# Attention scores of two query tiles at a time, in plain float32 on the two row halves of the array

## The chip, the cores and the metric

The kernel runs on one core of a Trainium2 chip. The metric is the device time of one execution in microseconds (us); less is better. Engines are named as in the profile: PE (matrix engine), PEld (its weight loads), DVE (vector), ACT (scalar), POOL (GpSimd), SP (the queue that issues nearly all DMAs).

## What is computed

One layer of a hybrid decoder in float32, for a prompt of 2048 positions and a small sample group. The change is in the prompt's attention: 8 heads of 64 channels; each position looks at keys at distances 0, d, 2d, ... in three branches, each with a softmax of its own, and the branches are merged by their denominators.

```python
BRANCHES = ((128, 1), (512, 4), (2048, 16))      # (window, dilation)
...
s = jnp.einsum('bnqrhc,bnkrhc->bnrhqk', qb, kc).astype(jnp.float32)
s = s * (HEAD_DIM ** -0.5) + bias[None, None, None]
s = jnp.where(valid[None, :, None, None], s, NEG_INF)
lse = jax.nn.logsumexp(s, axis=-1)
p = jnp.exp(s - lse[..., None])
o = jnp.einsum('bnrhqk,bnkrhc->bnqrhc', p.astype(vc.dtype), vc)
...
w = jax.nn.softmax(jnp.stack(lses, axis=0), axis=0)
return jnp.sum(w[..., None] * jnp.stack(outs, axis=0).astype(jnp.float32), axis=0)
```

Before it stands one projection to q, k, v, u, g; behind it the output projection, a gated feed-forward block and norms.

## The kernel before

The program is written out in the order of a plan: `at(step, phase, fn)` registers a call, and calls run by step, then by phase (early, exp, low, scores, turn, mid, values, out, misc, store). Each engine works in the order in which the calls issue its instructions. The projection (steps 0 to 240) stores q and k transposed, as channels by positions, to `qk_d`; each of them is split into a high part, which is rounded for the fast matmul format, and a low rest (L360 on ACT, L361 on DVE), and both parts are stored (L366). Positions of q stand by residue: within a block of 128, those that agree modulo 4 are neighbours. Positions of k stand in their natural order.

The attention follows as a list of items, one per step, from step `B0` = 240 on: for each head 16 band items (a tile of 128 queries against the branches of dilation 1 and 4) and 4 strided items (four residues modulo 16 at once, dilation 16). The orders FIRST, OTHER and LAST say how they are mixed.

- `load_head` (L855) brings three tiles of 128 rows by 2048 per head (L862): `qh` (the high part of q twice), `k` (high part over low part), `ql` (the low part of q twice). `join_q` (L891) adds qh and ql into `qx`, in float32.
- A band item (`band_scores`, L901): near scores, 256 keys, by two matmuls of 128 rows in the fast format, qh and ql against k (L909); far scores, up to 96 keys at distance 4 for each of the four query residues, by four float32 matmuls on 32 columns of the array each (L911). Then the bias and the row's minimum on DVE (L918), the exponential on ACT (L923), three transposes on PE (L934), a copy out (L938 on ACT, L942 on DVE); per four tiles the products with the values (L958 near, L970 far), whose two column halves of the array serve two tiles each.
- A strided item: POOL gathers k and q into `sq` (L985, L986), four float32 matmuls (L994), bias and minimum on DVE (L999, L1001), subtraction on POOL (L1006), exponential on ACT (L1009), four transposes (L1018), values (L1030).
- When a head is done, `Stats` works out the weights of the merge (L1062 is its matmul), stores them (L1090), `merge_load` reads them back spread out over rows (L1104), and POOL merges the outputs in three steps (L1113, L1115, L1117). All this runs beside the items of the next head.

The bias table `b_d` is spread out in DRAM during the projection (`table_spread`, L502). Scores go to one of two buffers `ps_s` of two banks each, of which an item uses the first bank.

Of the kernel before, what the change touches and what calls it, by code (L numbers as in the profile page):

```python
# [13 lines left out]
OP = mybir.AluOpType  # L14
# [53 lines left out]
def hymba_step(ctx: ExitStack, tc: tile.TileContext, A: dict, O: dict):  # L68
# [43 lines left out]
    qk_d = dram.tile([2, 2, DA, T], F32, name="qk_d")  # L112
# [240 lines left out]
    def transposed_split(which, t):  # L353
        pt = zn[which, t]
        thl = zn[which, t] = pair_tile()
        h_, l_ = thl[:, 0], thl[:, 1]
        if which == 0:
            pt = pt.rearrange("p (a i r) -> p a r i", a=4, r=4)
            h_, l_ = (x.rearrange("p (a r i) -> p a r i", a=4, r=4) for x in (h_, l_))
        act.activation(h_, pt, AF.Copy)  # L360
        dve.tensor_sub(l_, pt, h_.bitcast(F32))  # L361
# [129 lines left out]
    def table(c0, n, dst):  # L491
# [3 lines left out]
        act.activation(l_, pt[0:H, 0:n], AF.Copy, scale=-1.0)  # L495
        sync.dma_start(dst, l_)
        if c0 == 0:
            f_ = zn_tile()[0:H, 0:P]
            act.activation(f_, pt[0:H, 3:n:4], AF.Copy, scale=-1.0)
            sync.dma_start(lf_d, f_)  # L500

    def table_spread():  # L502
        for r in range(4):
            rows = slice(r * 32, r * 32 + 32)
            sync.dma_start(b_d[:, rows, 0:FAR], dap(lf_d, 31, [[P, H], [-1, 32], [1, FAR]]))
            sync.dma_start(b_d[:, rows, FAR:BAND], dap(l12_d, 511 - r, [[768, H], [-4, 32], [1, 2 * P]]))
        sync.dma_start(b_d[:, :, BAND:BW], dap(l3_d, 127, [[256, H], [-1, P], [1, P]]))
# [198 lines left out]
    at(70, "turn", table, 0, 512, l12_d[:, 0:512])  # L706
    at(71, "turn", table, 512, 256, l12_d[:, 512:768])
# [139 lines left out]
    def load_values(n, pair, by_residue, n0=0, n1=NT):  # L847

        if by_residue:
            src = dap(v_d, pair * 2 * C, [[NT * DA, P], [DA, NT], [1, 2 * C]])  # L850
        else:
            src = dap(v_d, pair * 2 * C + n0 * P * DA, [[DA, P], [P * DA, n1 - n0], [1, 2 * C]])
        sync.dma_start(n[:, n0:n1].rearrange("p n z c -> p n (z c)"), src)

    def load_head(h):  # L855
# [3 lines left out]
        for nm, w_, parts in (("qh", 0, (0, 0)), ("k", 1, (0, 1)), ("ql", 0, (1, 1))):  # L859
            t_ = d[nm] = qk.tile([P, T], F32R, name=nm, tag="qk", bufs=4)  # L860

            sync.dma_start(t_.bitcast(F32), dap(qk_d, ((w_ * 2 + parts[0]) * DA + h * C) * T,  # L862
                                                [[T, C], [(parts[1] - parts[0]) * DA * T, 2], [1, T]]))
            yield
        d["qx"] = qk.tile([P, T], F32, name="qx", tag="qk", bufs=4)
# [25 lines left out]
    def join_q(h, x, eng):  # L891
        qh, ql, q = (heads[h][nm][:, x * 512:(x + 1) * 512] for nm in ("qh", "ql", "qx"))
        eng.tensor_add(q, qh.bitcast(F32), ql.bitcast(F32))

# [6 lines left out]
    def band_scores(it):  # L901
        d, n = it["d"], it["n"]
        m = min(3, max(0, n - 1))
        near = P if n == 0 else 2 * P
        s = ps_s()[:, 0, :]
        c0 = FAR - 32 * m if n else FAR + P
        k0, f0 = (n + 1) * P - near, (n - 1 - m) * P
        for z, q in ((0, "qh"), (1, "ql")):
            pe.matmul(s[:, BAND - near:BAND], d[q][:, n * P:(n + 1) * P], d["k"][:, k0:k0 + near], start=(z == 0), stop=(z == 1))  # L909
        for r in range(4 if m else 0):  # L910
            pe.matmul(s[r * 32:r * 32 + 32, c0:FAR], d["qx"][:, n * P + r * 32:n * P + r * 32 + 32],  # L911
                      d["k"].bitcast(F32)[:, f0 + r:f0 + r + (32 * m - 1) * 4 + 1:4], start=True, stop=True)
# [68 lines left out]
    def strided_order(h, r4):  # L981

        d = heads[h]
        d["sq", r4] = t_ = ap_.tile([P, 2, 4, P], F32, name="sq", tag="sq", bufs=2)
        pool.tensor_copy(t_[:, 0], d["k"].bitcast(F32).rearrange("p (i r) -> p r i", r=NT)[:, r4 * 4:r4 * 4 + 4])  # L985
        pool.tensor_copy(t_[:, 1].rearrange("p b (n i) -> p b n i", i=8),  # L986
                         d["qx"].rearrange("p (n b i a) -> p b n i a", b=4, i=8, a=4)[:, :, :, :, r4])
# [1559 lines left out]
```

## Time and profile before

| | |
|---|---|
| median of 3 runs | 2467.68 us (2467.61 to 2467.91) |
| the profiled execution, its time | 2464.45 us |
| its span | 2462.6 us |
| mean granted clock of PE in the span | 0.986 |
| HBM read, written | 421.49 MB, 177.38 MB |
| projection | to about 567 us |
| attention of the 8 heads | about 567 to 869 us |
| the rest | about 869 us to the end |

The profile shows one execution. An engine's busy time is the union of its instructions; PE's is near the whole span, so the reader has to look at single items and at what ended the idle time of PE. "Idle before" in a group names who released the engine. The matmul rows hold modelled ends: what one costs is read from start to start. SPq rows are the issues of DMAs, not their transfers.

### The profile page before, as it was taken

Reading aid. Unit: us, or ns where it says so; the run is one execution under the profiler, and the core shown is the slowest. Engines: PE = TensorE matmul, PEld = TensorE weight load, DVE = VectorE, ACT = ScalarE, POOL = GpSimd, SP = SyncE. Lnnn points to the kernel's source line nnn. Section 1 sums busy time; section 2 is a strip of 40 time slices with the busy share of each in tenths; the row PEclk is TensorE's granted clock in tenths of the full one; section 3 lists DMA queues with packets and bytes.
Section 4 is the critical chain, followed back from the end, with each engine's and each line's share of the span. In section 5 each row is a group of like instructions: output and inputs, shape, how many; then the busy total and the mean of one; then the engine's idle time right before and its main releaser. Section 6 shows DMA issues by size and latency. Waiting matters only on the chain. (4 is left out here: it accounts for less than half of the span.)

```text
span 2462.6 us, 42576 instructions
## 1 busy us (share of the span) xinstructions
PE 2385.6 (97%) x14844; PEld 2053.9 (83%) x14844; DVE 1535.3 (62%) x2995; ACT 1204.5 (49%) x2766; POOL 1488.1 (60%) x1196
## 2 busy tenths in 40 slices
PE   8999999999999899999999999999999998999998
PEld 6877786667777678999999988999999977999997
DVE  3468673215666534767777676566666666677676
ACT  6424333224555546666655546444434446555555
POOL 2116553112766737888788764766566663888885
PEclk9999999999999998999999999999999999999999
DMA  9874757887888464787877654767666644877552
GB/s 289 272 230 147 233 158 225 249 285 211 230 219 238 113 199 136 248 267 223 264 248 225 216 160 144 266 201 223 203 212 211 206 136 154 279 246 249 173 169 88
DMA packets 355938, 519.84 MB, mean 211 GB/s; under 512 B 35783, under 2 KB 198784, under 8 KB 350476
## 3 DMA queue, kind: packets, MB, share of 16 engines
q1 hardware_dynamic: 348876, 505.07, 65.5%
q10 hardware_dynamic: 6848, 12.06, 1.7%
q8 instruction: 117, 1.92, 0.3%
q14 instruction: 97, 0.79, 0.1%
HBM read 421.49 MB, written 177.38 MB: 243 GB/s over the span
## 5 line engine op out<-in xcount | busy, mean ns | idle before, releaser
L1664 POOL TENSOR_TENSOR op<-fr,op 128x512 fp32r<-128x512 f32 x392 | 522.4, 1343 | 348.8 <-ACT op L1660 257.5
L1901 PE MATMUL ps_m<-xh,op 128*128 128x384 f32 (+3 forms) x1344 | 429.0, 319 | 4.9 <-DVE raw L1912 3.6
L1902 PE MATMUL ps_m<-xl,op 128*128 128x384 f32 (+3 forms) x1344 | 427.4, 318 | 2.5 <-POOL xl L145 2.5
L1903 PE MATMUL ps_m<-xh,op 128*128 128x384 f32 (+3 forms) x1344 | 427.9, 318 | 0.0
L1754 DVE TENSOR_TENSOR acc<-acc,ps_o 128x512 f32<-128x512 f32 x448 | 300.0, 683 | 72.5 <-PE ps_o L1752 65.2
L1752 PE MATMUL ps_o<-hop 128*128 128x512 f32 x1142 | 322.6, 394 | 1.7 <-DVE hop L1733 1.0
L1901 PEld LDWEIGHTS ps_m<-xh,op 128*128 128x128 f32 x1344 | 255.6, 190 | 14.2 <-DVE raw L1912 6.8
L1902 PEld LDWEIGHTS ps_m<-xl,op 128*128 128x128 f32 x1344 | 255.5, 190 | 8.0 <-POOL xl L145 2.8
L1903 PEld LDWEIGHTS ps_m<-xh,op 128*128 128x128 f32 x1344 | 255.2, 190 | 0.0
L1752 PEld LDWEIGHTS ps_o<-hop 128*128 128x128 f32 x1142 | 209.4, 188 | 37.7 <-DVE hop L1733 2.8
L1660 ACT ACTIVATE op<-fr 128x512 fp32r<-128x512 f32 x396 | 239.5, 621 | 0.0
L325 PE MATMUL ps_s<-wh,xh 128*128 128x512 f32 x480 | 198.0, 413 | 6.4 <-ACT xh L142 6.0
L326 PE MATMUL ps_s<-wl,xh 128*128 128x512 f32 x480 | 191.0, 398 | 0.7 <-DVE wl L233 0.7
L327 PE MATMUL ps_s<-wh,xl 128*128 128x512 f32 x480 | 190.9, 398 | 0.0
L1901 PE MATMUL ps_t<-xh,op 128*128 128x384 f32 (+2 forms) x560 | 180.4, 322 | 6.1 <-ACT xh L1550 3.2
L1902 PE MATMUL ps_t<-xl,op 128*128 128x384 f32 (+2 forms) x560 | 179.5, 321 | 0.7 <-DVE xl L1572 0.7
L1903 PE MATMUL ps_t<-xh,op 128*128 128x384 f32 (+2 forms) x560 | 179.8, 321 | 0.0
L553 POOL TENSOR_TENSOR pr<-kv,qb 96x512 f32<-96x512 f32 x32 | 48.0, 1501 | 169.3 <-DMA kv<-in_cache_k_dram 67.7
L1733 POOL TENSOR_TENSOR hop<-hop 128x512 fp32r<-128x512 f32 x96 | 131.0, 1365 | 11.5 <-ACT hop L1729 6.5
L325 PEld LDWEIGHTS ps_s<-wh,xh 128*128 128x128 f32 x480 | 91.8, 191 | 43.0 <-issue 18.0
L1752 PE MATMUL ps_m<-hop 128*128 128x512 f32 x384 | 119.4, 392 | 0.0
L1901 PEld LDWEIGHTS ps_t<-xh,op 128*128 128x128 f32 x560 | 106.6, 190 | 10.8 <-ACT xh L1550 3.8
(573 smaller groups left out, 5557.6 us busy)
## 6 DMA issues: line engine op xcount, KB each, us to landing
fr<-ab_d SPq DMA_DIRECT2D x308, 256.0 KB
hop<-dd_d SPq DMA_DIRECT2D x143, 256.0 KB
out_ks_dram<-in_cache_k_dram SPq DMA_DIRECT2D x56, 512.0 KB
out_vs_dram<-in_cache_v_dram SPq DMA_DIRECT2D x56, 512.0 KB
ab_d<-fr SPq DMA_DIRECT2D x88, 256.0 KB
dwx<-dd_d SPq DMA_DIRECT2D x71, 256.0 KB
qk_d<-pair SPq DMA_DIRECT2D x64, 256.0 KB
ab_d<-pair SPq DMA_DIRECT2D x63, 256.0 KB
```

Of the source, the lines that this page charges most:

```text
L325: pe.matmul(o[j], xh[:, k, :], wh, start=(k == 0), stop=False)
L326: pe.matmul(o[j], xh[:, k, :], wl, start=False, stop=False)
L327: pe.matmul(o[j], xl[:, k, :], wh, start=False, stop=(k == KD - 1))
L553: eng.tensor_mul(pr[0:n], x[0:n], q[0:n])
L1660: act.activation(ops[f, j][0], ab[f][j], AF.Copy)
L1664: (pool if f > 1 or j in POOL_LOW[f] or B.b0 else dve).tensor_sub(lo_, ab[f][j], hi.bitcast(F32))
L1733: (pool if B.b0 or k >= 7 * (NF // 2 - 1) else dve).tensor_sub(lo_, lo_.bitcast(F32), hi.bitcast(F32))
L1752: pe.matmul(ps, l_, r_, start=(new and y == 0), stop=(y == 2), skip_group_check=True)
L1754: dve.tensor_add(x[:, cs], x[:, cs], ps)
L1901: pe.matmul(out, wh[:, ks], xh[:, :, k], start=(k == 0 and q not in (2, 4, 6)), stop=False, skip_group_check=True)
L1902: pe.matmul(out, wh[:, ks], xl[:, :, k], start=False, stop=False, skip_group_check=True)
L1903: pe.matmul(out, wl[:, ks], xh[:, :, k], start=False, stop=(k == 3), skip_group_check=True)
```

## The change

Exact q and k of 64 channels are stored once (`qk_d` is half as large; L360 stays as a copy, L361 goes), both by residue. A head loads two tiles, q and k, each with its 64 channels twice, on rows 0 to 63 and 64 to 127. `pair_scores` issues the scores of two neighbouring tiles: the even tile on the rows 0 to 63 of the array and into the first bank of `ps_s`, the odd one on the rows 64 to 127 and into the second bank. The near scores are one float32 matmul per tile (256 keys), the far scores four. A strided item puts its four matmuls on the two halves in turn, with two banks; its bias takes two DVE instructions. `join_q` goes. As k now stands by residue, the columns of the bias table and the rows of the near values do too: the table is spread by 36 smaller transfers, one per step, and a natural-order value load takes four DMAs instead of one. The bias of an even tile comes right before that of the odd one, the transposes of both come one step later than before, and the groups' value products two steps later; the tile `e` gets 6 buffers instead of 3.

```diff
-        thl = zn[which, t] = pair_tile()
-        h_, l_ = thl[:, 0], thl[:, 1]
...
-        act.activation(h_, pt, AF.Copy)
-        dve.tensor_sub(l_, pt, h_.bitcast(F32))
+        zn[which, t] = x = pair_tile(F32)[:, 0]
+        act.activation(x.rearrange("p (a r i) -> p a r i", a=4, r=4), pt.rearrange("p (a i r) -> p a r i", a=4, r=4), AF.Copy)
...
-    at(75, "misc", table_spread)
+    for j in range(36):
+        at(84 + j, "misc", table_spread, j // 9, j % 9 - 1)
...
-            src = dap(v_d, pair * 2 * C + n0 * P * DA, [[DA, P], [P * DA, n1 - n0], [1, 2 * C]])
...
+        for r in range(4):
+            src = dap(v_d, (n0 * P + r) * DA + pair * 2 * C, [[4 * DA, 32], [P * DA, n1 - n0], [1, 2 * C]])
+            sync.dma_start(n[r * 32:r * 32 + 32, n0:n1], src)
...
-        for nm, w_, parts in (("qh", 0, (0, 0)), ("k", 1, (0, 1)), ("ql", 0, (1, 1))):
-            t_ = d[nm] = qk.tile([P, T], F32R, name=nm, tag="qk", bufs=4)
...
+        for w_, nm in enumerate("qk"):
+            t_ = d[nm] = qk.tile([P, T], F32, name=nm, tag="qk", bufs=2)
+            sync.dma_start(t_, dap(qk_d, (w_ * DA + h * C) * T, [[0, 2], [T, C], [1, T]]))
             yield
-        d["qx"] = qk.tile([P, T], F32, name="qx", tag="qk", bufs=4)
...
-        for z, q in ((0, "qh"), (1, "ql")):
-            pe.matmul(s[:, BAND - near:BAND], d[q][:, n * P:(n + 1) * P], d["k"][:, k0:k0 + near], start=(z == 0), stop=(z == 1))
-        for r in range(4 if m else 0):
-            pe.matmul(s[r * 32:r * 32 + 32, c0:FAR], d["qx"][:, n * P + r * 32:n * P + r * 32 + 32],
-                      d["k"].bitcast(F32)[:, f0 + r:f0 + r + (32 * m - 1) * 4 + 1:4], start=True, stop=True)
...
+    def pair_scores(*its):
+
+        d, s = its[0]["d"], ps_s()
+        for z, it in enumerate(its):
+            n = it["n"]
+            m = min(3, max(0, n - 1))
+            near = P if n == 0 else 2 * P
+            it.update(s=s[:, z, :], c0=FAR - 32 * m if n else FAR + P, m=m)
+            half = slice(z * C, z * C + C)
+            k0 = (n + 1) * P - near
+            pe.matmul(it["s"][:, BAND - near:BAND], d["q"][half, n * P:(n + 1) * P], d["k"][half, k0:k0 + near], start=True, stop=True)
+        for r in range(4):
+            for z, it in enumerate(its):
+                n, m, half = it["n"], it["m"], slice(z * C, z * C + C)
+                if m:
+                    k = d["k"][half].rearrange("p (n r i) -> p n r i", r=4, i=32)[:, n - 1 - m:n - 1, r, :]
+                    c = n * P + r * 32
+                    pe.matmul(it["s"][r * 32:r * 32 + 32, it["c0"]:FAR].rearrange("p (n i) -> p n i", i=32),
+                              d["q"][half, c:c + 32], k, start=True, stop=True)
...
+            half = slice(a % 2 * C, a % 2 * C + C)
+            pe.matmul(s[:, a % 2, a // 2 * P:(a // 2 + 1) * P], t_[half, 1, a], t_[half, 0, a], start=True, stop=True)
...
-        dve.tensor_tensor(e, s.rearrange("p (a b) -> p a b", a=4), d["b3"].unsqueeze(1).broadcast_to([P, 4, P]), op=OP.add)
+        for y in range(2):
+            dve.tensor_tensor(e[:, 2 * y:2 * y + 2], s[:, y], d["b3"].unsqueeze(1).broadcast_to([P, 2, P]), op=OP.add)
...
-    LAST = [0, "s", 1, "s", 2, "s", 3, "s", 4, 5, 6, 7] + list(range(8, NT))
+    LAST = ["s", 0, 1, "s", 2, 3, "s", 4, 5, "s", 6, 7] + list(range(8, NT))
...
-                grp["y"] = (4, 5, 6) if h in (0, H - 1) else (4, 6, 7)
+                grp["y"] = (4, 5, 6) if h == H - 1 and n == NT - 1 else (6, 7, 8)
...
-        at(x + 1, "scores", bias, it)
+        if it["kind"] == "s" or n % 2:
+            at(x + 1, "scores", bias, it)
+        else:
+            x += 1 if items[i + 1]["kind"] == "b" else 2
+            at(x + 1, "low", bias, it)
```

How the order moves on PE, in the middle of a head (`e` holds probabilities, `ps_t` and `ps_o` are banks for transposes, `sq` is the strided copy). Before:

```order
L909 MATMUL ps_s<-k,qh 128x256
L909 MATMUL ps_s<-k,ql 128x256
L911 MATMUL ps_s<-k,qx 32x96 x4
L1018 MATMUL ps_t_5680<-ident,e_5583 128x128 x4
L934 MATMUL ps_t_5687<-ident,e 128x128 x3
L994 MATMUL ps_s<-sq 128x128 x4
L934 MATMUL ps_o_5705<-ident,e 128x128 x3
L909 MATMUL ps_s<-k,qh 128x256
L909 MATMUL ps_s<-k,ql 128x256
L911 MATMUL ps_s<-k,qx 32x96 x4
L934 MATMUL ps_t_5722<-ident,e 128x128 x3
```

The same place on PE in the changed kernel (L899 near, L906 far, L1015 and L928 transposes, L964 far values, L989 strided scores):

```order
L899 MATMUL ps_s<-k,q 128x256 x2
L906 MATMUL ps_s<-k,q 32x96 x8
L1015 MATMUL ps_o_5702<-ident,e_5625 128x128 x4
L964 MATMUL ps_o_5672<-pt,vf 64x32 x8
L989 MATMUL ps_s<-sq 128x128 x4
L928 MATMUL ps_t_5747<-ident,e 128x128 x3
L928 MATMUL ps_t_5752<-ident,e 128x128 x3
L899 MATMUL ps_s<-k,q 128x256 x2
L906 MATMUL ps_s<-k,q 32x96 x8
L928 MATMUL ps_o_5780<-ident,e 128x128 x3
L928 MATMUL ps_t_5785<-ident,e 128x128 x3
```

The scores of two tiles now stand together, half tiles in turn, and so do the six transposes of two tiles.

On DVE, between two strided items of a head (ISA rows are the bias with the minimum and the reading of that minimum). Before:

```order
L999 TENSOR_TENSOR e_6230<-ps_s,b 128x512
L1001 TENSOR_REDUCE st<-e_6230 128x4
L918 ISA e,st<-ps_s,b 128x352
L918 ISA st 128x1
L942 COPY pt<-ps_t_6273 128x384
L918 ISA e,st<-ps_s,b 128x352
L918 ISA st 128x1
L893 TENSOR_TENSOR qx<-qh,ql 128x512
L918 ISA e,st<-ps_s,b 128x352
L918 ISA st 128x1
L1013 TENSOR_REDUCE st<-e_6230 128x4
```

The same place in the changed kernel (L912 bias, L996 and L998 strided bias and minimum, L1010 strided sum, L936 copy):

```order
L996 TENSOR_TENSOR e_5625<-ps_s,b 128x256 x2
L998 TENSOR_REDUCE st<-e_5625 128x4
L936 COPY pt<-ps_o_5634 128x384
L912 ISA e,st<-ps_s,b 128x352
L912 ISA st 128x1
L912 ISA e,st<-ps_s,b 128x352
L912 ISA st 128x1
L936 COPY pt<-ps_t_5668 128x384
L1010 TENSOR_REDUCE st<-e_5625 128x4
```

The join has left DVE's order, the strided bias is two instructions, and the biases of two tiles follow each other.

More of the change, by code (lines that the diff above doesn't have):

```diff
@@ L109, in ps_a @@
         return bank(turn[2])
-    qk_d = dram.tile([2, 2, DA, T], F32, name="qk_d")
+    qk_d = dram.tile([2, DA, T], F32, name="qk_d")
     v_d = dram.tile([T, DA], F32, name="v_d")
@@ L489, in table_loads, with table @@
         sync.dma_start(tb["12"][0:33, 768:1024], A["oh3"])
-    def table(c0, n, dst):
+    def table(c0, n, dst, by=1):
         pt = ps_t()
@@ L494, in table, with table_spread @@
         l_ = zn_tile()[0:H, 0:n]
[L495 to L507, printed above, removed]
+        act.activation(l_.rearrange("p (r y) -> p r y", r=by), pt[0:H, 0:n].rearrange("p (y r) -> p r y", r=by), AF.Copy, scale=-1.0)
+        sync.dma_start(dst, l_.rearrange("p (r y) -> p r y", r=by) if by > 1 else l_)
+    def table_spread(qr, kr):
+        rows = slice(qr * 32, qr * 32 + 32)
+        if kr < 0:
+            sync.dma_start(b_d[:, rows, 0:FAR], dap(l12_d, 3 * 192 + 31, [[768, H], [-1, 32], [1, FAR]]))
+            sync.dma_start(b_d[:, rows, BAND:BW], dap(l3_d, 127 - qr * 32, [[256, H], [-1, 32], [1, P]]))
+            return
+        base = 511 - qr + kr % 4 + kr // 4 * P
+        c0 = FAR + kr // 4 * P + kr % 4 * 32
+        sync.dma_start(b_d[:, rows, c0:c0 + 32], dap(l12_d, base % 4 * 192 + base // 4, [[768, H], [-1, 32], [1, 32]]))
     def sample_table_load():
@@ L705, in hymba_step @@
     at(62, "misc", table_loads)
[L706 to L707 removed]
+    at(70, "turn", table, 0, 512, l12_d[:, :, 0:128], 4)
+    at(71, "turn", table, 512, 256, l12_d[:, :, 128:192], 4)
     at(72, "turn", table, 768, 256, l3_d)
     at(73, "misc", sample_table_load)
[L710 removed]
+    for j in range(36):
+        at(84 + j, "misc", table_spread, j // 9, j % 9 - 1)
     at(82, "turn", sample_table)
@@ L1156, in scores @@
         it.update(d=heads[it["h"]], st=sts[it["h"]]["t"])
-        (strided_scores if it["kind"] == "s" else band_scores)(it)
+        if it["kind"] == "s":
+            strided_scores(it)
+        elif it["n"] % 2 == 0:
+            it["grp"]["first"] = it
+        else:
+            pair_scores(it["grp"]["first"], it)
     def bias(it):
         (strided_bias if it["kind"] == "s" else band_bias)(it)
-    FIRST = list(range(8)) + ["s", 8, 9, "s", 10, 11, "s", 12, "s", 13, 14, 15]
+    FIRST = list(range(8)) + ["s", 8, 9, "s", 10, 11, "s", "s", 12, 13, 14, 15]
     OTHER = [0, 1, "s", 2, 3, 4, 5, "s", 6, 7, 8, 9, "s", 10, 11, 12, 13, "s", 14, 15]
-    LAST = [0, "s", 1, "s", 2, "s", 3, "s", 4, 5, 6, 7] + list(range(8, NT))
+    LAST = ["s", 0, 1, "s", 2, 3, "s", 4, 5, "s", 6, 7] + list(range(8, NT))
     items, taken = [], set()
@@ L1182, in hymba_step @@
                 grp["x"] = B0 + len(items) - 1
-                grp["y"] = (4, 5, 6) if h in (0, H - 1) else (4, 6, 7)
-                taken.update(range(grp["x"] + 4, grp["x"] + grp["y"][2] + 1))
+                grp["y"] = (4, 5, 6) if h == H - 1 and n == NT - 1 else (6, 7, 8)
+                taken.update(range(grp["x"] + grp["y"][0], grp["x"] + grp["y"][2] + 1))
     NI = len(OTHER)
@@ L1187, in hymba_step @@
     at(222, "misc", begin, 0)
-    for y in (222, 224, 226, 228):
+    for y in (222, 224, 226):
         at(y, "misc", load, 0)
@@ L1258, in hymba_step @@
         at(x + 2, "exp", band_exp, it)
-        at(x + 3, "turn", band_turn, it)
-        at(x + 4, "low", low_parts, it)
+        o = 3 if h == H - 1 and n > 11 else 4
+        at(x + o, "turn", band_turn, it)
+        at(x + o + 1, "low", low_parts, it)
         if n % 4 == 3:
@@ L1264, in hymba_step @@
             at(x + it["grp"]["y"][2], "early", band_out, it)
-    for x in range(4):
-        at(232 + 2 * x, "out", join_q, 0, x, pool)
-        for h in range(1, H):
-            at(B0 + (h - 1) * NI + 10 + 2 * x, "store", join_q, h, x, dve)
     for G in range(1, 4):
```

49 lines of the change are left out of this document (16 added, 33 removed).

## The prediction

> **What bounds the kernel now.** I read the page's busy table first, then the busy time by stretch, to find the stage that the change touches.
>
> ```profile
> PE 2385.6 (97%) x14844; PEld 2053.9 (83%) x14844; DVE 1535.3 (62%) x2995; ACT 1204.5 (49%) x2766; POOL 1488.1 (60%) x1196
> ```
> ```profile
> 567.00:869.00 302.00, 290.84 (x3746) 217.14 (x3745) 196.45 (x535) 164.46 (x472) 186.20 (x195) 0.99 0.71 197
> 640.00:680.00 40.00, 39.10 (x535) 29.18 (x531) 26.95 (x81) 20.97 (x63) 26.19 (x28) 1.00 0.70 215
> ```
> The columns after the length are PE, PE's weight loads, DVE, ACT, POOL, granted clock, DMA share, GB/s. TensorE is busy all through; the attention of the eight heads fills 567 to 869 us, with 290.8 of 302 us on PE. In a middle stretch PE idles 0.9 of 40 us, and DVE, the next, has 13 us free. All later stages stand behind this one in PE's order, so a microsecond taken from PE here is taken from the span, until another engine is late.
>
> Next I read PE's timeline inside one head, to price one item of each kind from start to start. It merges records of one line. (A plain-float32 matmul has two records: the far product x4 in program order is x8 here.)
>
> ```profile
> 643.03 1.13 PE L970 MATMUL ps_o<-pt,vf 96*64 96x32 f32 x32
> 644.08 0.39 PE L909 MATMUL ps_s<-k,qh 128*128 128x256 f32 x1
> 644.30 0.28 PE L909 MATMUL ps_s<-k,ql 128*128 128x256 f32 x1
> 644.51 0.53 PE L911 MATMUL ps_s<-k,qx 128*32 128x96 f32 x8
> 644.97 0.66 PE L1018 MATMUL ps_t<-ident,e 128*128 128x128 f32 x4
> 645.47 0.49 PE L934 MATMUL ps_t<-ident,e 128*128 128x128 f32 x3
> 645.79 1.06 PE L994 MATMUL ps_s<-sq 128*128 128x128 f32 x8
> 646.69 0.49 PE L934 MATMUL ps_o<-ident,e 128*128 128x128 f32 x3
> ...
> 651.83 1.23 PE L970 MATMUL ps_o<-pt,vf 32*64 32x32 f32 x16
> 652.99 0.39 PE L909 MATMUL ps_s<-k,qh 128*128 128x256 f32 x1
> ```
> One band item costs 644.97 - 644.08 = 0.89 us of PE: near scores 0.43, far scores 0.46. One strided item costs 646.69 - 645.79 = 0.90 us.
>
> **The scores on PE, the term that decides.** The new near product is one float32 matmul per tile, two passes of 256 columns. The strided rows give the price of a float32 pass: 0.90 us / 8 = 0.112 us for 128 columns, so 0.225 for 256. If the two row halves run side by side, a pair's near part is 2 x 0.225 = 0.45, plus 0.11 of waiting for the first weights (the qh record lasts 0.39, the ql record 0.28). From ql's start to the first far record pass 0.21 us, the stream of ql and the switch from wide to narrow tiles together, so the switch lies between 0 and 0.21; I take 0.09. The far part is bounded from these rows:
>
> ```profile
> L911 PE MATMUL ps_s<-k,qx 128*32 128x96 f32 x768 | 50.7, 343 | 0.0
> L994 PE MATMUL ps_s<-sq 128*128 128x128 f32 x256 | 34.7, 278 | 0.5 <-POOL sq L986 0.5
> L1030 PE MATMUL ps_o<-eT,v 128*64 128x64 f32 x512 | 21.9, 228 | 0.3 <-ACT o L1040 0.3
> L911 PE MATMUL ps_s<-k,qx 128*32 128x64 f32 x64 | 3.3, 287 | 0.0
> L911 PE MATMUL ps_s<-k,qx 128*32 128x32 f32 x64 | 2.4, 228 | 0.0
> ```
> L911 grows by (343 - 228) / 64 = 1.8 ns a column, the strided pass costs 0.112 / 128 = 0.87, and 64 columns at L1030 last no longer than 32 at L911. L911 reads every fourth key; the changed kernel reads runs of 32 neighbours. If the stride is what slows it, two passes of 96 columns save 2 x 96 x 0.9 ns = 0.17 us: 0.29 instead of 0.46. High end: 0.46 as now for all eight tiles together, if four narrow tiles at once are the cause. L911 has the tile shape, L1030 the read pattern; I take the middle, rounded up, 0.40.
>
> A full pair: 0.11 + 0.45 + 0.09 + 0.40 = 1.05 us (0.94 to 1.11) against 2 x 0.89 = 1.78, a saving of 0.73 (0.67 to 0.84). Six of a head's eight pairs are full: 48 x 0.73 = 35 us. The pair of tiles 2 and 3 has short far parts, about 0.55 saved: 8 x 0.55 = 4. Tiles 0 and 1 have none, 0.1: 1 us. A strided item becomes two float32 passes of 128 columns, twice: 0.45, plus weights 0.11 and a switch in and out, 0.1 to 0.2: 0.70, saving 0.20 (0.14 to 0.34): 32 x 0.20 = 6. Together 46 us off PE (40 to 57).
>
> That two halves of the array overlap, the trace shows for column halves: L970 needs 652.99 - 651.83 = 1.16 us for 16 records when one half works, and 1.05 for 32 when both do. For row halves it has no row. [...]
>
> **Removed from DVE, POOL, SP.**
>
> ```profile
> L893 DVE TENSOR_TENSOR qx<-qh,ql 128x512 f32<-128x512 f32 x28 | 25.7, 919 | 0.0
> L999 DVE TENSOR_TENSOR e<-ps_s,b 128x512 f32<-128x512 f32 x32 | 21.8, 680 | 0.4 <-PE ps_s L994 0.3
> L942 DVE COPY pt<-ps_o 128x256 f32<-128x256 f32 x7 | 3.0, 425 | 0.9 <-PE ps_o L934 0.6
> L361 DVE TENSOR_TENSOR pair<-ps_t,pair x24: 672/691/694, 36.0 to 523.1; 128x512 fp32r<-128x512 f32 x24
> ```
> ```profile
> 8.00:567.00 559.00, 543.52 (x2533) 414.61 (x2534) 278.50 (x511) 201.51 (x332) 184.07 (x129) 0.98 0.76 233
> ```
> The 28 joins leave DVE (25.7 us); the strided bias becomes two instructions of 256 columns, by the 425 ns row 32 x (0.85 - 0.68) = 5 us more. DVE then has 196 - 26 + 5 = 175 us in a stage of about 256: 69% as against 65%, still below PE. The split of q and k in the projection (32 times 0.69 us) goes too; it was hidden behind PE, which works 543.5 of 559 us there, and its ACT copy stays. Half the stores of q and k (8 MB) and a third of their loads (1 MB a head) go. Added are 27 table transfers and three more issues per value load, all on SP. The table rows are written about 300 us before they are read, and SP is no row's releaser in the stage: nothing on the path (0 to 2 us).
>
> **What is late next.** A shorter stage uncovers chains that don't shorten. The tightest is the merge of the head before.
>
> ```profile
> POOL ob L1113 <- DMA pair<-f_d: 20.4, 5, 6.6
> ```
> ```profile
> 639.53 0.57 SPq L862 DMA_DIRECT2D ql<-qk_d  x1
> 644.72 3.66 SPq L1090 DMA_DIRECT2D f_d<-f  x4
> 653.55 2.80 SPq L1104 DMA_DIRECT2D pair<-f_d  x4
> ```
> ```profile
> 658.66 0.97 POOL L1113 TENSOR_TENSOR ob<-ob,pair 128x256 f32<-128x256 f32 x1 [6.34 <-DMA pair<-f_d]
> 659.60 0.89 POOL L1115 TENSOR_TENSOR o<-o,pair 128x256 f32<-128x256 f32 x1
> 660.57 0.86 POOL L1117 TENSOR_TENSOR ob<-ob,o 128x256 f32<-128x256 f32 x1
> 661.39 1.04 POOL L1006 TENSOR_TENSOR e<-e,st 128x512 f32<-128x512 f32 x1
> ```
> ```profile
> 640.37 0.62 PE L1062 MATMUL ps_t<-sel_r,sm 128*128 128x16 f32 x4
> 663.14 0.66 PE L1018 MATMUL ps_t<-ident,e 128*128 128x128 f32 x4 [0.39 <-ACT e L1009]
> ```
> The weights of the merge are written (L1090), read back spread out (L1104) and wait for the transfers issued before them; the first merge starts at 658.66, and behind its three instructions on POOL stands L1006, on which the strided item's exp and then its transposes on PE (663.14) depend. PE already waits 0.39 us. Between 640.37 and 663.14 PE's work falls by six pairs and two strided items, 6 x 0.73 + 2 x 0.2 = 4.8 us, so if this chain keeps its length PE would wait 4.4 us more. But three loads of 1 MB stand ahead of it in the queue (the last issued at 639.53); with one gone, at the 215 GB/s of this stretch, it can start up to 4.9 us sooner. So 0 to 4.4 us a head, times the six middle heads, under whose strided items such a merge runs: 0 to 26. I take 1.3 a head, 8 us, nearer the low end, because the bytes removed sit right in front of the chain. The scores' two buffers are no new wait: between a pair and the next use of its buffer PE has 0.50 + 1.05 + 0.70 + 0.66 = 2.9 us of other work, and the two biases need 1.2 on DVE. In the last head, whose chain has little PE work to hide it, pairing delays the first of two biases by one item: 1 us (0 to 3).
>
> **Sum.** 46 - 8 - 1 + 1 (the projection's lighter DMA, 0 to 2) = 38 us. The profiled execution took 2464.45 us (span 2462.6 and 1.85 around it), so the changed one about 2426; the median of the runs shown, 2467.68, is 3.2 above the profiled execution, so I predict 2430.
>
> **Rivals.**
> The halves don't overlap (the one on the slower side). Its place is L906 and L899 of the new kernel: if a matmul on one row half waits for that on the other, a pair costs 0.11 + 4 x 0.225 near, 0.09, and 16 far passes of 0.08 to 0.17 us in turn: 2.4 to 3.8 us instead of 1.78, and a strided item 1.1 to 1.2 instead of 0.9. That is 48 x 0.6 to 2.0 plus 32 x 0.25, 37 to 104 us lost: about 2535. It decides as soon as a full pair needs over 1.78. For it: no matmul of 64 rows stands in the trace. Against it: the column halves overlap in L970, and the two row halves write different banks. Chance 0.1.
>
> The overlap is partial. If the two passes of an instruction kept their place in program order, the second half's first pass would wait for the first half's second: three passes instead of two, 64 x 0.225 = 14 us more near, and 4 us more in the strided items. Then 46 - 18 - 5 = 23 us, 2445. Against it: L911's four column tiles have two passes each; one after another but for one pass of overlap they would need five passes of 0.17 us, 0.87, and they take 0.46. [...] Chance 0.08.
>
> The stage becomes bound by its chains: PE does shrink by 46 us, but the merge chain gives nothing back (26 lost) and DVE, at 69%, delays one strided item in each head by 0.75 us (6 us): 46 - 32 = 14, 2454. For it: POOL and DVE release most of what PE waits for here, and in-order queues make a delay in one a delay in all. Chance 0.15.
>
> No change: it needs the two bounds at their worst together with the merge chain and DVE both at theirs; 0.02.
>
> **Chances.** The forecast, overlap of both halves and small new waits, 2430: 0.65; 2445: 0.08; 2454: 0.15; no change 0.02; slower 0.10. The range takes in the low end of the sum (57 off PE, no new wait: 2410) and the chain-bound case (2456). A measurement of this kernel tells about 0.2% (5 us) from no change: faster 0.87, same 0.03, slower 0.10.
>
> **What will show it.** On PE's timeline of the changed kernel, a full pair (L899 x4, L906 x16 records) should take 0.94 to 1.11 us to the next line's start, and a strided item (L989 x8) 0.56 to 0.76; the stage from the first L899 to the last far value should be about 264 instead of 302 us, with PE still busy over 92% of it; no join on DVE; the merge's wait on POOL shorter than 6.3 us and PE's wait on L1015 under 2 us a head. I am wrong if the pair takes over 1.4 us (partial or no overlap), or if PE's busy share in the stage falls below 88% (chains).

## The result, and the profile after

The changed kernel takes 2709.74 us (median of 4 runs, 2704.36 to 2714.2), the kernel before 2467.80 us beside it: 1.098 times as long (95% interval 1.095 to 1.100), 242 us slower where 38 us faster was forecast. The profiled execution took 2707.78 us, its span is 2706.0 us. One of the four executions of e7_before_halves, among the experiments below, took 4634 us; the ratio given there is made without it.

The busy time of one stretch, inside the attention stage in both kernels, first of the kernel before, then of the changed one (columns: length, PE, PE's weight loads, DVE, ACT, POOL, granted clock, DMA share, GB/s):

```profile
567.00:836.00 269.00, 263.59 (x3460) 198.49 (x3459) 181.05 (x488) 150.79 (x435) 166.39 (x174) 1.00 0.72 202
```
```profile
567.00:836.00 269.00, 144.59 (x1726) 104.04 (x1726) 79.00 (x240) 71.91 (x207) 67.31 (x72) 0.73 0.35 97
```

No engine is the bound any more: PE idles 124 of 269 us, all other engines idle more than before, and the DMA engines, the only other candidate, are busy 0.35 of the time and move half as much. The last far value of the stage starts at 1107.7 us instead of 865.7: the loss is all here. What the engines wait for in it (the waits of the changed kernel, 567 to 1110 us; total, times, longest):

```profile
POOL ob L1110 <- DMA pair<-f_d: 225.5, 9, 42.8
DVE pt L936 <- PE ps_t L928: 155.9, 10, 34.6
ACT ob L972 <- DMA cat_d<-ob: 150.9, 5, 34.9
PE ps_o L928 <- ACT e L917: 146.0, 5, 33.9
POOL sq L980 <- DMA k<-qk_d: 64.5, 2, 53.9
```

Three of the five end with a DMA, and the longest of each last 35 to 54 us. One of them, followed back through SP's timeline, then ACT's, then PE's:

```profile
852.33 1.07 SPq L856 DMA_DIRECT2D q<-qk_d  x1
853.45 2.88 SPq L856 DMA_DIRECT2D k<-qk_d  x1
856.43 39.96 SPq L887 DMA_DIRECT2D vf<-v_d  x4
896.50 1.21 SPq L1119 DMA_DIRECT2D cat_d<-ob  x2
```
```profile
903.70 0.38 ACT L972 ACTIVATE ob<-ps_o 128x256 f32<-128x256 f32 x1 [33.17 <-DMA cat_d<-ob]
```
```profile
872.12 0.40 PE L906 MATMUL ps_s<-k,q 64*32 64x96 f32 x16
904.70 0.69 PE L928 MATMUL ps_o<-ident,e 128*128 128x128 f32 x2 [32.18 <-ACT e L917]
```

The two loads of q and k are issued at 852 to 856. The four loads behind them, 0.77 MB, keep SP's queue for 39.96 us (four such issues took 3.1 us before), and only then comes the store of the merged rows (L1119), for whose buffer ACT waits 33.17 us, and behind ACT the exponentials and PE. The loads of q and k are therefore the thing to look at. For most of the 30 us from 660 on nothing but such a pair of loads is running (the DMA view of that window, 40 slices of 0.75 us):

```profile
DMA  1111112111111111157211111121111211111211
GB/s 66 44 66 44 66 44 76 55 44 66 44 66 44 44 66 66 66 85 285 65 44 55 55 44 66 44 76 55 44 66 45 81 44 44 66 44 66 60 44 66
q1 hardware_dynamic: 626, 1.82, 16.3%
```

The share is 0.1 to 0.2, which is 2 of 16 engines, and 44 to 66 GB/s. By the trace's packet records the 256 pieces of 8 KB of a head (2 MB) take 0.32 us each, as little as before (0.36), but two at a time: 256 / 2 x 0.32 = 41 us, and 41 us is how long they last there (655.5 to about 697). Two at a time is the rule for them: of the time from 567 to 900 us in which such packets run, they run two at a time for 93%, against all sixteen engines at once for 44% in the kernel before. The source of the new load is `[[0, 2], [T, C], [1, T]]`: its outermost dimension (the first pair of step and count) has 2 steps, that of the old one 64.

PE's own rows, one pair and one strided item of the changed kernel:

```profile
862.64 0.72 PE L989 MATMUL ps_s<-sq 64*128 64x128 f32 x8
863.29 0.55 PE L928 MATMUL ps_t<-ident,e 128*128 128x128 f32 x3
863.67 0.49 PE L928 MATMUL ps_o<-ident,e 128*128 128x128 f32 x3
864.09 0.70 PE L899 MATMUL ps_s<-k,q 64*128 64x256 f32 x4
864.72 0.40 PE L906 MATMUL ps_s<-k,q 64*32 64x96 f32 x16
865.05 0.87 PE L928 MATMUL ps_t<-ident,e 128*128 128x128 f32 x6
865.86 0.34 PE L1027 MATMUL ps_o<-eT,v 128*64 128x64 f32 x4
```

A pair takes 865.05 - 864.09 = 0.96 us (two items took 1.78), its near part 0.63, its far part 0.33; a strided item 0.65 us (0.90 before). The six transposes that follow a pair take 0.81, where two times three took 0.32 to 0.33 each.

### The profile page after: what moved, and what is told of

It reads as the page before. It is cut to its first block, busy times and chain, and to the rows that moved or that the text cites. A ratio compares the mean times of both kernels' runs of the same rounds, so it can differ in the third digit from the quotient of the medians.

```text
span 2706.0 us, 42496 instructions
## 1 busy us (share of the span) xinstructions
PE 2391.3 (88%) x14844; PEld 2049.2 (76%) x14844; DVE 1493.5 (55%) x2967; ACT 1204.0 (44%) x2765; POOL 1471.4 (54%) x1192
## 5 line engine op out<-in xcount | busy, mean ns | idle before, releaser
L1755 PEld LDWEIGHTS ps_o<-hop 128*128 128x128 f32 x1142 | 209.4, 188 | 37.7 <-DVE hop L1736 2.8
L928 PE MATMUL ps_o<-ident,e 128*128 128x128 f32 x135 | 29.7, 336 | 147.0 <-ACT e L917 146.0
L1110 POOL TENSOR_TENSOR ob<-ob,pair 128x256 f32<-128x256 f32 x26 | 19.0, 732 | 225.5 <-DMA pair<-f_d 225.5
L928 PEld LDWEIGHTS ps_o<-ident,e 128*128 128x128 f32 x135 | 18.8, 169 | 151.9 <-ACT e L917 147.1
L545 POOL TENSOR_TENSOR pr<-kv,qb 96x512 f32<-96x512 f32 x32 | 43.1, 1346 | 159.8 <-DMA kv<-in_cache_k_dram 83.8
```

Source lines behind the costliest of these rows:

```text
L928: pe.transpose(pt[:, i * P:(i + 1) * P], e[:, a:a + P], ident)
L1755: pe.matmul(ps, l_, r_, start=(new and y == 0), stop=(y == 2), skip_group_check=True)
```

## The experiments

Each ratio is against the kernel before, run beside it on the same chip. The runs of one kernel lie up to 23 us apart (those of the kernel before, 2455 to 2474 on these chips), so beside the time I give the stage itself in the profiled execution: from the first near product's weights to the last one's, and from head to head (heads 0 to 6). These are of one execution each: that of f1 was the slowest of its ten (2479.35 us), that of f4 the fastest of its ten (2452.08), so small differences between two rows prove little.

| kernel | time, us | ratio (95%) | stage, us | heads, us |
|---|---|---|---|---|
| before | 2467.68 | 1 | 281.9 | 30.6 36.4 35.5 34.4 35.5 34.4 34.4 |
| after | 2709.74 | 1.098 (1.095-1.100) | 494.8 | 60.3 59.5 71.5 61.1 74.2 61.4 75.8 |
| e1_wide_loads | 2474.24 | 1.0038 (1.0026-1.0049) | 287.7 | 32.1 30.3 46.0 30.2 43.2 29.4 43.8 |
| e2_before_narrow | 2861.53 | 1.161 (1.158-1.163) | 634 | 86 79 90 80 90 80 89 |
| e3_one_half | 2493.85 | 1.0124 (1.0096-1.0152) | 312.7 | 48.9 36.0 39.6 34.9 43.1 34.9 37.6 |
| e4_three_engines | 2592.83 | 1.0518 (1.0494-1.0541) | 389.6 | 43.5 45.1 55.7 47.7 60.3 44.6 59.6 |
| e5_stored_twice | 2470.21 | 1.0018 (1.0003-1.0033) | 275.8 | 32.2 30.3 39.6 29.4 41.7 29.4 40.4 |
| e6_values_too | 2466.52 | 1.0011 (0.9994-1.0028) | 269.5 | 34.1 30.3 33.7 29.4 35.9 32.4 38.4 |
| e7_before_halves | 2504.30 | 1.0150 (1.0133-1.0167) | 319.8 | 37.8 36.4 40.8 34.5 48.7 35.6 45.7 |
| f1_merges_later | 2465.40 | 1.0008 (0.9986-1.0029) | 273.9 | 32.2 30.3 37.1 30.7 38.3 30.7 39.6 |
| f2_subtract_on_vector | 2473.26 | 1.0025 (1.0007-1.0043) | 271.8 | 31.2 31.4 37.6 30.4 36.4 34.1 39.8 |
| f3_far_values_early | 2459.86 | 0.9970 (0.9951-0.9988) | 269.0 | 32.6 37.6 30.8 29.6 37.9 29.6 37.9 |
| f4_both | 2459.56 | 0.9981 (0.9959-1.0003) | 262.8 | 32.1 38.9 30.7 30.7 30.4 30.4 33.3 |
| f5_all_repairs | 2454.69 | 0.9962 (0.9947-0.9978) | 270.1 | 32.7 31.0 37.7 30.7 33.8 31.9 38.0 |
| f6_repairs_one_half | 2488.39 | 1.0115 (1.0085-1.0145) | 301.9 | 30.6 44.4 34.9 45.7 34.9 34.9 37.6 |
| g1_before_merges_later | 2465.96 | 1.0007 (0.9996-1.0018) | 279.9 | 30.6 36.4 34.5 34.5 35.3 34.4 34.5 |

### The loads of q and k

e1_wide_loads, the changed kernel with each load in two of 64 rows:

```diff
-            sync.dma_start(t_, dap(qk_d, (w_ * DA + h * C) * T, [[0, 2], [T, C], [1, T]]))
+            for z in range(2):
+                sync.dma_start(t_[z * C:(z + 1) * C], dap(qk_d, (w_ * DA + h * C) * T, [[T, C], [1, T]]))
```


> The changed kernel with one thing altered: each head's q and k (1 MB each) are loaded by two transfers of 64 rows of 8 KB instead of one whose slowest dimension is the 2 copies. Theory A (the loads run on 2 DMA engines and everything behind them waits): the 8 KB packets run 16 at a time instead of 2, the stage of the heads falls from about 550 us to about 265, and the time is 2430 us (2410 to 2456), the sum of the prediction. Theory B (pairing made chains on ACT, DVE and POOL that PE waits for, and the DMA waits are their result): PE's waits for exp and for POOL stay, the time stays above 2600. In between, 2460 to 2600, both have a share.

2474.24 us, 10 us above the kernel before beside it (2463.81): this one line carries some 232 of the 242 us. But it doesn't reach the forecast; see below.

e2_before_narrow, the kernel before with the two dimensions of its load exchanged, so that the outermost has 2 steps:

```diff
-                                                [[T, C], [(parts[1] - parts[0]) * DA * T, 2], [1, T]]))
+                                                [[(parts[1] - parts[0]) * DA * T, 2], [T, C], [1, T]]))
```


> The kernel before with the dimensions of its qh, k and ql loads exchanged, so that the slowest is the 2 copies (rows land in another order, the same for q and k, so the sums are the same). Theory A: 3 MB a head on 2 DMA engines, 384 packets of 8 KB at 0.31 us each / 2 = 60 us a head against 35 us of work: eight heads near 480 us or more instead of 282, so 2650 to 2750 us. Theory B: the loads are hidden by the head's work, 2468 within 15 us.

2861.53 us (ratio 1.161, 1.158 to 1.163), more than expected: it has three such loads a head, not two. The scores are the old ones, so the loads alone do it (columns as above):

```profile
567.00:700.00 133.00, 63.70 (x442) 45.94 (x442) 21.50 (x55) 17.89 (x48) 19.37 (x18) 0.67 0.31 98
```

e4_three_engines, e1 with the 64 rows cut into 51 and 13:

```diff
-            for z in range(2):
-                sync.dma_start(t_[z * C:(z + 1) * C], dap(qk_d, (w_ * DA + h * C) * T, [[T, C], [1, T]]))
+            for z in range(2):
+                for c0, c1 in ((0, 51), (51, C)):
+                    sync.dma_start(t_[z * C + c0:z * C + c1], dap(qk_d, (w_ * DA + h * C + c0) * T, [[T, c1 - c0], [1, T]]))
```


> The kernel of e1_wide_loads with each 64-row transfer cut into 51 and 13 rows. If the number of engines is the largest divisor up to 16 of the slowest dimension (51 = 3 x 17, 13), the 51 rows run on 3 engines and a head's q and k hold these for 4 x 17 packets x 0.31 = 21 us, under the 30 us of a head's work, but whatever is spread over all engines waits for its share on these three. Theory A: 8 KB packets run mostly 3 at a time; time between e1_wide_loads and the changed kernel, nearer the former: 2450 to 2560. If the engine count doesn't depend on divisors (rows dealt out one by one): same as e1_wide_loads within 10 us.

2592.83 us (1.0518, 1.0494 to 1.0541), 119 us above e1 with the same bytes to the same rows. So it is not the zero stride of the source: an outermost dimension of 51 slows the load too, and by less than one of 2. The packet records show why: pieces of 8 KB run three at a time for 75% of the time in which any runs (567 to 900 us), where they ran two at a time for 93% in the changed kernel and for 96% in e2, and on all sixteen at once for over half of it in e1. So outermost dimensions of 2, 51 and 64 went with two, three and sixteen packets at a time, the numbers that the expectations of e1 and e4 supposed; that a divisor decides in other loads too is not shown.

### Row halves, and what still keeps e1 from the forecast

e3_one_half, e1 with both tiles of a pair, and all strided items, on rows 0 to 63:

```diff
-            half = slice(z * C, z * C + C)
+            half = slice(0, C)
```
(and likewise for the far and the strided products)

> The kernel of e1_wide_loads with both tiles of a pair, and all four matmuls of a strided item, on row half 0 of the array (banks as before). It takes the overlap of the halves away and nothing else. If the halves overlap fully: near scores of a pair grow from 2 passes of 0.21 us to 4, far scores by about 0.2, a full pair from 0.96 to about 1.6 us, a strided item from 0.65 to about 0.88: 56 x 0.6 + 32 x 0.23 = 41 us more than e1_wide_loads, some of it hidden where PE waited, so 30 to 45 more. If the halves did not overlap at all: no difference to e1_wide_loads (under 5 us).

2493.85 us (1.0124, 1.0096 to 1.0152), 20 us above e1 and less than expected: from 567 to 836 us PE idles 30 of 269 us in e1 and 4 in e3, so the longer products fill idle time. What e1 waits for, 500 to 900 us:

```profile
POOL ob L1111 <- DMA pair<-f_d: 44.9, 10, 14.8
ACT e L1007 <- POOL e L1004: 55.4, 27, 6.9
PE ps_t L1016 <- ACT e L1007: 14.0, 8, 3.4
```

It is the chain that the prediction priced: merge weights late, POOL held, the strided item's subtraction behind it, its exponential, its transposes. It isn't all of PE's idle time, though; PE's own waits in e1, 567 to 836 us, by what ended them:

```profile
PE ps_t L1016 <- ACT e L1007: 12.6, 7, 3.4
PE ps_o L929 <- ACT e L918: 5.8, 3, 2.2
PE ps_o L1028 <- DMA v<-v_d: 4.5, 1, 4.5
```

The chain ends 12.6 of the 30 us. The second line is a band item's exponential, which stands on ACT behind a copy that waits for the store of merged rows. The heads show the lateness more plainly: odd heads take 29.4 to 30.3 us, 4 to 6 less than before, even ones 43 to 46. The next runs look for what makes the weights late.

e5_stored_twice writes q and k twice, so that one load of 128 different rows brings a head; e6_values_too adds a second copy of v in the order of the band, for one load instead of four.

```diff
-        sync.dma_start(qk_d[which, :, t * P:(t + 1) * P].rearrange("(a p) t -> p a t", p=P), x)
+        for p0, p1, r0 in ((0, P, C), (0, C, 0), (C, P, 3 * C)):
+            sync.dma_start(dap(qk_d, (which * 2 * DA + r0) * T + t * P, [[T, p1 - p0], [4 * C * T, 4], [1, P]]), x[p0:p1])
...
-            sync.dma_start(t_, dap(qk_d, (w_ * DA + h * C) * T, [[0, 2], [T, C], [1, T]]))
+            sync.dma_start(t_, dap(qk_d, (w_ * H + h) * 2 * C * T, [[T, P], [1, T]]))
... (and in e6)
+        sync.dma_start(dap(vr_d, t * P * DA, [[DA, 32], [32 * DA, 4], [1, DA]]), zn["v", t])
...
+        sync.dma_start(n[:, n0:n1], dap(vr_d, n0 * P * DA + pair * 2 * C, [[DA, P], [P * DA, n1 - n0], [1, 2 * C]]))
```


> The changed kernel, with q and k written to DRAM twice per head (16 MB of stores, as the kernel before has), so that a head's q or k is one load of 128 different rows. Theory A (the two loads of 64 rows in the previous run are slow because each of them lands in one half of SBUF's partitions: 8 KB packets took 0.58 to 0.65 us there against 0.32 to 0.39 before): the packets take under 0.4 us again, the issue of the merge's weights comes earlier, the wait of POOL on the merge's weights falls from 44.9 us to under 30, and the time falls from 2474 to 2450 to 2465. Theory B (the chain of the merge is late because the scores are shorter, whatever the loads): 2470 to 2480. Theory C (the transposes behind half-height matmuls eat the gain on TensorE): 2470 to 2480, and TensorE idles no less than 35 us in the stage.

> The previous kernel, and v also written a second time with the rows of a tile sorted by residue, so that the values of the band are one load of 128 partitions instead of four of 32. Theory A: 512-byte packets, 0.05 to 0.07 us in the stage with four loads, take 0.04 again, even heads become as short as odd ones (30 us from start to start), and the time is 2430 to 2445, what was predicted for the change. Theory B: no difference of more than 5 us to the previous kernel. Theory C: the same.

e7_before_halves, the kernel before with its loads cut into two of 64 rows:

```diff
-            sync.dma_start(t_.bitcast(F32), dap(qk_d, ((w_ * 2 + parts[0]) * DA + h * C) * T,
-                                                [[T, C], [(parts[1] - parts[0]) * DA * T, 2], [1, T]]))
+            for z in range(2):
+                sync.dma_start(t_.bitcast(F32)[z * C:(z + 1) * C], dap(qk_d, ((w_ * 2 + parts[0]) * DA + h * C + z * 32) * T,
+                                                [[T, 32], [(parts[1] - parts[0]) * DA * T, 2], [1, T]]))
```


> The kernel before, with each of its three loads of q and k a head cut into two of 64 rows, the first into partitions 0 to 63, the second into 64 to 127; same bytes, same rows, 16 DMA engines each. Theory A: 8 KB packets take about 0.6 us instead of 0.35, 384 packets a head on 16 engines then cost each engine 6 us more a head; the stage's DMA share rises from about 0.75 to 0.9, the wait of POOL on the merge's weights rises above 30 us, and the time is 5 to 40 us longer. Theory B and C: within 5 us of before.

Packets of 8 KB took, on average from 567 to 836 us, 0.36 us before, 0.60 in e1, 0.61 in e7, 0.35 in e5: a load into partitions 0 to 63, or 64 to 127, was slower by 0.25 us a packet though it had all 16 engines. It isn't the cutting of the load: in e4, cut further, the packets that ran three at a time into the same partitions took 0.33 us. In the kernel before this costs 38 us (e7). Why a load into one such half was slower, no run here shows. Repairing it in the changed kernel takes the even heads from 43 to 46 us to 40 to 42 (e5) and, with the values in one load too, 34 to 38 (e6), and the stage from 287.7 to 275.8 and 269.5 us, 12 less than before. The time follows only to 2466.52 us, within 0.2% of before: in e6 the stage began 14 us later, at 581.6 instead of 567.6. The stores that it adds may be one reason; how large, these runs don't tell, since in e5, with most of them, it began at 570.3, and in f1 to f4, with the same projection as e5, at 573 to 586.

f1 to f4 start from e5. f1 puts the merges three items later, f2 the subtraction L1004 on VectorE, f3 loads the far values a head earlier into six buffers, f4 is f1 and f3.

```diff
-            for ch, (a, b) in enumerate(((8, 11), (8, 14), (11, 17), (11, 24) if ahead else (11, 20))):
+            for ch, (a, b) in enumerate(((8, 11), (8, 14), (11, 17), (11, 24)) if ahead else ((8, 14), (8, 17), (11, 20), (11, 23))):
...
-        pool.tensor_sub(e, e, m.unsqueeze(2).broadcast_to([P, 4, P]))
+        dve.tensor_sub(e, e, m.unsqueeze(2).broadcast_to([P, 4, P]))
...
-        heads[h]["vf"][G] = x = hv.tile([FAR, 4, 4, 2 * C], F32, name="vf", tag="vf", bufs=3)
+        far.setdefault(h, {})[G] = x = hv.tile([FAR, 4, 4, 2 * C], F32, name="vf", tag="vf", bufs=6)
```


> The kernel that stores q and k twice (2470 us; its even heads take 40 us from start to start, its odd ones 29.4), with the merge of each head but the last two three items later (and its store). Theory D (TensorE waits in the even heads because POOL, in order, waits for the weights of the merge, which come late): the merge's weights are there when POOL gets to them, the wait of POOL on them falls under 10 us, even heads take 32 to 36 us, the time 2445 to 2458. Theory E (the strided items' own chain bias, subtract, exp is what is late, and the merge only stands beside it): within 5 us of 2470.

> The same kernel with the subtraction of the strided items' maximum (32 instructions of 1.04 us on POOL) on VectorE, so that the exp of a strided item does not stand behind the merge on POOL. Theory D: the merge may wait without TensorE; even heads 31 to 35 us, 2440 to 2458. Theory E: VectorE, which has the bias of the next items queued behind it, gets the work instead: 2465 to 2490.

> The same kernel with six buffers for the far values instead of three, and each pair of heads' three loads of them (768 KB in 512-byte pieces, the longest pieces of the chain that ended last) issued one head earlier, out of the way of the merge's weights. Theory D with these loads as the cause of the lateness: f_d is written and read back some 5 us earlier in the even heads, they take 31 to 35 us, the time is 2440 to 2455. If the lateness comes from the DMA engines as a whole (0.7 to 0.9 busy in the stage), the loads only delay something else: 2462 to 2475.

> Far values early and merges later together. Theory D: all heads but the first and last at 29.5 to 31 us, 2430 to 2445, below the kernel before. Otherwise no better than the better one of the two.

f1 and f2, at 2465 and 2473 us, differ from e5 by no more than the runs scatter; theory D said more, and their even heads still take 36 to 40 us. In f1 the merge's chain is out of the way as theory D has it: POOL waits 8.1 us for the weights from 500 to 900 us instead of 32.4 in e5. But PE then waits elsewhere (567 to 836 us):

```profile
PE ps_o L929 <- ACT e L918: 12.0, 3, 4.9
PE ps_s L900 <- DVE st L913: 4.8, 5, 1.0
PE ps_o L1028 <- DMA v<-v_d: 4.7, 1, 4.7
PE ps_t L1016 <- ACT e L1007: 1.1, 2, 0.7
```

The first line stands behind the store of the merged rows, now later too, for which ACT waits 14.9 us. So the merge's chain is one late thing among several, and moving it alone uncovers the next. f3 takes 10 us off. In f4, which has f1's and f3's changes, heads 2 to 5 take 30.4 to 30.7 us, even or odd alike, but in one execution, the fastest of its ten; its time is that of f3, so that it needs both changes is not shown. What f4 still loses lies mostly in heads 0 and 1, and before the stage. Its time missed the 2430 to 2445 expected.

f5_all_repairs has one copy of q and k in DRAM again, each tile loaded in three pieces (rows 32 to 95 at once, so that both halves are written), the schedule of f4 with two of the far-value loads later still, and the sample's transposes later; f6 is f5 on one row half; g1 is the kernel before with the merges of f1.

```diff
+            for p0, p1, c0 in ((32, 96, 0), (0, 32, 32), (96, P, 0)):
+                sync.dma_start(t_[p0:p1], dap(qk_d, (w_ * DA + h * C + c0) * T, [[T, p1 - p0], [1, T]]))
```


> Single copy of q and k in DRAM again (no added stores, as in the changed kernel); each head's q and k come in three loads, 64 rows into partitions 32 to 95 and 32 rows into each end, so that half of the rows go to both halves of SBUF at once; far values a head early in six buffers (the second pair's last two groups one head later still), merges three items later, and the sample rows' transposes five items later. Theory D (what is lost on top of the two-engine loads is late DMA in front of POOL's merge, not TensorE): the scores from the first to the last near product take 255 to 262 us (281.9 in the kernel before, 262.8 with q and k stored twice), the time 2440 to 2455, a ratio of 0.990 to 0.996. If the 64-row loads cost as much as two halves did: even heads over 35 us, 2460 to 2475.

> The previous kernel with both tiles of a pair, and all strided items, on row half 0. The overlap of the two row halves alone: 64 pairs whose near part takes four passes instead of two (0.33 us more a pair in the changed kernel's rows, 0.63 against 0.959 start to start being the near part and the whole) and far parts twice as long (0.33), 32 strided items 0.3 us more: 30 to 50 us more on TensorE, so 30 to 50 us more in time if TensorE is the bound again; 20 or less, as in the earlier run with the merge late, if it isn't.

> The kernel before with the same shift of the merges by three items, as a control: TensorE idles 1 us in 40 there, so there is little to gain: within 5 us of before. If it gains over 8 us, the repaired kernel's gain is not the change's.

f5 takes 2454.69 us, 0.4% less than the kernel before (0.9962, 0.9947 to 0.9978), the best of these kernels and at the upper edge of the 2440 to 2455 expected. The control g1 gains nothing, so the merges' shift is worth nothing without the change; the earlier far values and the later sample transposes were not tried without it. The stage of f5 (270.1 us) missed the 255 to 262: the packets take 0.54 us again, and the later merge makes the wait seen in f1, for the merged rows' store (640 to 680 us):

```profile
ACT ob L975 <- DMA cat_d<-ob: 5.8, 1, 5.8
PEld ps_o L931 <- ACT e L920: 5.0, 1, 5.0
```

f6 costs 34 us more than f5, though its four executions lie between 2476 and 2496. PE in f6 is full (267.6 of 269 us from 567 on, against 239.7 in f5), and its rows show what the second half is worth:

```profile
663.91 1.16 PE L992 MATMUL ps_s<-sq 64*128 64x128 f32 x8
665.00 0.55 PE L931 MATMUL ps_o<-ident,e 128*128 128x128 f32 x3
665.38 0.49 PE L931 MATMUL ps_t<-ident,e 128*128 128x128 f32 x3
665.80 1.13 PE L902 MATMUL ps_s<-k,q 64*128 64x256 f32 x4
666.86 0.55 PE L909 MATMUL ps_s<-k,q 64*32 64x96 f32 x16
667.35 0.55 PE L931 MATMUL ps_t<-ident,e 128*128 128x128 f32 x3
```

On one half a pair takes 1.55 us and a strided item 1.09; on two, 0.96 and 0.65.

## Why the prediction was wrong, point by point

**The step that failed** is the one on the loads: "Half the stores of q and k (8 MB) and a third of their loads (1 MB a head) go", nothing on the path, "0 to 2 us". It counted the bytes that go, at the 215 GB/s of the stretch, and gave the two new loads no price; what it left out is on how many engines a load runs, two of 16 here. The old and new patterns stand in the diff, `[T, C]` outermost in one and `[0, 2]` in the other. At 41 us a head for its two loads, eight heads cannot be done in the 264 us forecast, and the later DMAs of SP's queue wait with them. e1 and e2 show both directions. None of the rivals had it: the one on the slower side put the loss on PE.

**TensorE's terms held.** A full pair was forecast at 1.05 us (0.94 to 1.11) and takes 0.96; the near part 0.65 and 0.63; the far part was taken at 0.40 between the ends 0.29 and 0.46 and takes 0.33, as if the stride explained most of what slowed L911 (the number of rows changed with it, so this isn't shown); a strided item 0.70 (0.56 to 0.76) and 0.65. The halves overlap: the first passes of the two tiles start 7 ns apart in the trace, the second ones 0.32 us later, and f6 shows the price without. The rival of no overlap had its price wrong: 2.4 to 3.8 us a pair, where f6 needs 1.55, below the old 1.78 (its far part takes 0.55, not 1.3 to 2.7), and f6 as a whole lies 25 us above the kernel before beside it, not 67.

**The sum on PE came out, by two errors that cancel.** The six transposes behind a pair take 0.81 us, not twice 0.33, a cost that the prediction didn't have, while a pair and a strided item save more than forecast. Here is the stage of the profiled executions, from the first near product to the last far value, in us. An interval at half the granted clock is counted as half work and half loss, an estimate; it gives the same scores in e1, f4 and f5 (58.0, 58.1, 58.1 for near and far).

| | stage | PE's work at full clock | scores, transposes in it | lost by the clock | PE idle |
|---|---|---|---|---|---|
| before | 298.1 | 284.2 | 132, 61 | 2.8 | 11.2 |
| after | 510.9 | 235.6 | 78, 68 | 48.5 | 226.8 |
| e1 | 307.1 | 237.8 | 79, 69 | 31.2 | 38.1 |
| f4 | 282.9 | 238.5 | 79, 69 | 19.4 | 25.0 |
| f5 | 290.8 | 240.2 | 79, 70 | 18.2 | 32.3 |
| f6 | 316.8 | 281.4 | 125, 66 | 32.3 | 3.1 |

In e1, f4 and f5 the scores give 53 us and the transposes take 8 to 10 back: 44 to 46 off PE, where 46 was forecast. That the sum agrees this well is luck. The second row half alone is worth 41 us of this work (f6 against f5).

**The give-back was mis-sized, and one term was missing.** "I take 1.3 a head, 8 us", 0 to 26, for the merge's chain. In e1 PE idles 27 us more in the stage than before, in f5 21. The chain is the one described (L1111, L1004, L1007, L1016), but by the waits above it ends less than half of e1's idle time. The argument that it "can start up to 4.9 us sooner" with one load gone did not hold: in e1 the weights of head 1 are stored 21.9 us after head 2 begins (10.4 before) and read back at 27.8 (19.3). The even heads run with the far values' loads ahead of them in the queue, and the stage still moves most of the old bytes: 50.1 MB from 567 to 836 us in f5, 54.4 before. The clock had no term in the prediction, and costs 28 us more than before in e1 and 15 in f5. So of 44 to 46 us less work nothing is left in e1, and 7 in f5.

**The other outcome named there**, the stage bound by its chains at 2454, is where the repaired kernel ends: 2454.69. That the numbers agree is luck: f5 has changes of schedule that the forecast kernel hadn't, its stage begins 7 us earlier (560.7 instead of 567.6), and its losses are late DMAs and the clock more than DVE (4 of PE's 29 us of waits from 567 to 836 us). The mark "PE's busy share in the stage falls below 88%" was the right one to name: over the stage as the prediction bounds it, the share is 96% before, 56% after the change, 87.6% in e1 and 89% in f5.

What stays open: why the transposes take longer beside half-height tiles (in f6 too, on one row half); how much the added stores of e5 and e6 cost the projection; why f5's stage begins 7 us earlier than e1's, with the same projection; and why the far values' loads slow even the heads where they are not waited for.

## What to carry to other kernels

Before pricing a load by its bytes, read the outermost dimension of its source's pattern: here a 2, a 51 and a 64 went with two, three and sixteen packets at a time, and behind one pair of slow loads four issues kept their queue for 39.96 us. Two halves of the array are worth having for plain float32 of 64 channels (34 us here, more than all that the repaired kernel gains), but where PE is 97% busy, shortening its work first uncovers the chains that it covered, one behind the other; move their loads and their late steps in the same change. A stage's length from head to head helps to tell such causes apart where the total time, with its spread of 20 us, does not; one execution of each kernel is little to go by.

## What the runs showed of the hardware that I had not expected

**Short waits came with half the clock, and cost about twice their length.** Busy time of e1 in steps of 5 us, around the wait of 3.05 us in head 2:

```profile
655.00:660.00 5.00, 3.22 (x44) 2.15 (x42) 2.28 (x7) 1.90 (x6) 0.00 (x0) 0.77 0.27 79
660.00:665.00 5.00, 2.37 (x32) 1.34 (x28) 0.00 (x0) 0.27 (x1) 3.70 (x5) 0.84 0.97 222
665.00:670.00 5.00, 4.58 (x47) 3.97 (x48) 1.98 (x7) 3.93 (x12) 4.92 (x7) 0.50 0.34 114
670.00:675.00 5.00, 5.00 (x49) 3.41 (x49) 3.37 (x10) 2.75 (x8) 4.55 (x5) 0.53 0.19 46
675.00:680.00 5.00, 5.00 (x74) 3.99 (x70) 2.06 (x8) 2.59 (x10) 3.12 (x5) 1.00 1.03 223
```

PE idles 4.4 us from 655 to 665, and then the granted clock is 0.50 for 10 us: 4.8 us lost, as much as the waits. Over e1's stage PE idles 38 us and loses 31 by the clock, in the kernel before 11 and 3 (table above). By the trace's clock records, e1's stage has twelve stretches of half clock: seven of 3.4 us, three of 6.8 and two of 10.2, each behind 4 us in which PE idled 0.9 us or more. But f6 fell to 0.50 for 23.9 us from 690.9 on, with PE never idle in the 8 us before; its beginning:

```profile
690.00:695.00 5.00, 5.00 (x30) 3.64 (x34) 1.99 (x4) 2.91 (x8) 2.17 (x3) 0.59 1.16 307
695.00:700.00 5.00, 5.00 (x47) 3.68 (x40) 2.13 (x6) 1.63 (x5) 4.83 (x6) 0.50 1.10 202
700.00:705.00 5.00, 5.00 (x54) 3.55 (x53) 0.98 (x4) 0.60 (x1) 0.00 (x0) 0.50 0.84 112
```

Such stretches in heads 1 and 3 (17 and 24 us) make these take 44.4 and 45.7 us where most others take 34.9. What set off the long one, no run tells.

**Sixteen engines are not enough.** Loads into partitions 0 to 63 or 64 to 127 took 0.60 us a packet of 8 KB, loads into all 128 took 0.36, with the same engines and bytes; in a kernel whose stage has a DMA share of 0.72 that cost 38 us.
